# Moving the later modulation rows into the early stage, with raw weight blocks in two sets and side tokens loaded apart

## The chip, the cores and the metric

The kernel runs on one core of one Trainium2 chip. The metric is the device time in microseconds; lower is better. Before the change, three runs took 2741.22 to 2743.19 us, with a median of 2743.05. Another execution was profiled; it took 2743.47 us, and the profile's span, from its first to its last instruction, is 2741.7 us.

## The reference, cut to what matters

One layer of a diffusion trunk: an HGRN2 mixer (gated linear recurrence, both directions, 8 heads of 128) and a gated ConvFFN, each behind an RMSNorm that is modulated by rows made from `silu(c)`. 2048 latent tokens of width 1024, 256 context tokens.

```python
sc_lat, sc_ctx = jax.nn.silu(c), jax.nn.silu(c_ctx)
m_l = (sc_lat @ w_ada[l] + b_ada[l])[:, None, :]        # six rows of 1024
sh1, sc1, g1, sh2, sc2, g2 = jnp.split(m_l, 6, axis=-1)
hl = modulate(rmsnorm(lat, norm_g[l, 0]), sh1, sc1)
yc, yl = hgrn2_mixer(hc, hl, hg_w_in[j], ...)           # h @ w_in: q, f_fwd, f_bwd, i, g
lat = lat + g1 * yl
hl = modulate(rmsnorm(lat, norm_g[l, 1]), sh2, sc2)
lat = lat + g2 * conv_ffn(hl, ffn_w_up[l], ...)
return rmsnorm(lat, final_g)
```

The first two modulation rows (`sh1`, `sc1`) are needed at once. The change deals with the last four: `g1`, `sh2`, `sc2`, `g2`. `g1` is first needed in the mixer's second pass, where it scales the output weight; the others later.

## The kernel before, in words

The order of the instructions of each engine is drawn by a list scheduler at build time: an instruction that the text issues late can be put earlier on its queue when its operands and its place are free, loads above all. The text gives priorities through its order. It uses agendas: `at(when, f)` puts a step at a tick, and a tick passes with each three matmuls (one k step). Matrix products run with split operands: each fp32 factor is a high part (ScalarE, line 80) and a remainder (VectorE, line 81), and each k step multiplies high x high, high x low and low x high.

**Early stage** (`early()`, up to about 421 us). It makes the values (`ty` 3) and the output gates (`ty` 4) of all tokens by a Strassen-like scheme: seven products (`FACTORS`) for each pair of heads, of 12 matmuls each. `todo` is their order: 49 products over the second half of the tokens (`g` = 1 in the code), then, from `turn_over` on, 56 over the first half. A pair of heads is a `Heads` object: `prepare` loads the raw weight blocks (two of 512 KB, line 591), makes two sums on POOL (`sums`, lines 217 and 218) and splits the block that is needed, four products ahead (`LOOK`). Raw blocks lie in four first places (`rawp` twice, `Sf`, `Sb`), used once, and then in a ring of four in the pool `px`.

The token factors of the first half of the tokens come from `side_tokens`: four groups of two token tiles each are loaded (line 657), normalized (lines 130, 132), turned by TensorE (line 139), modulated on ScalarE (line 143), combined on VectorE and stored to `part_d` (line 664). All four groups use one tile, `side`; group j's load and norm are one step, at tick `c0 + 40 + 25 * j`, and its turns follow from 9 ticks later. `load_factor` (line 695) brings the parts back as factors into `fraw` and splits them. `turned_out` transposes a finished value (line 476) some ticks after its product and stores it.

**Mixer** (`mixer_scan()`, about 421 to 1250 us). Two passes over the 8 heads: the first over the first half of the tokens and the context, the second over the rest. Each unit projects gates and queries (lines 870 to 872), makes decay factors on VectorE, and steps the state (line 1070, VectorE) that TensorE reads for the outputs (line 1087).

The later modulation rows are a generator here, `ada_rest` (lines 1126 to 1154). For each of four rows it goes over 8 blocks of `w_ada` (512 KB each, line 1131), accumulates block x `silu(c)` on VectorE (lines 1143 and 1144), adds over partitions with two fp32 matmuls against ones (line 1151), and stores the row in `m_rows`. It steps 8 times in the second pass's first head and 6 times in each of the next five, each step tied behind the unit's last factor (`tied`). In heads 2 to 5, `gate1` and `out_scaled` (line 1170) make the scaled output weight from the first of these rows.

Of the kernel before, what the change touches and what calls it, by code (L numbers as in the profile page):

```python
# [21 lines left out]
D = 1024  # L22
# [23 lines left out]
def body(ctx, tc, a, out):  # L46
# [204 lines left out]
    def early():  # L251
# [143 lines left out]
        def then(f, *args):  # L395
            with behind_of(chain[-1]):
                chain.append(f(*args))
# [73 lines left out]
        def turned_out(o, dst, after=6):  # L471

            def turn():
                tr = z_tile("tr")
                for i in range(UT):
                    pe.transpose(tr[:, i], o[:, i], ident)
                act.activation(o, tr, AF.Copy)
                sp.dma_start(dst, o)

            at(clock[0] + after, turn)  # L480
# [8 lines left out]
        for k in range(KT):  # L489
            at(clock[0] + 36 + 4 * k, lambda k=k: then(unit0, k))  # L490
# [69 lines left out]
        raw_ring, raw_first = [], []  # L560

        def raw_tile():
            if len(raw_first) < 4:
                p, tag = ((rawp, "raw"), (rawp, "raw"), (hp, "Sf"), (hp, "Sb"))[len(raw_first)]
                raw_first.append(p.tile([128, 2, 4, 128], F32, name="raw", tag=tag,
                                        bufs=2 if p is rawp else 1))
                return raw_first[-1]
            if not raw_ring:
                raw_ring.extend([px.tile([128, 4, 2, 4, 128], F32, name="raw", tag="X", bufs=1), 0])
            raw_ring[1] += 1  # L570
            return raw_ring[0][:, (raw_ring[1] - 1) % 4]

        class Heads(Blocks):

            def __init__(self, ty, h):
                super().__init__(ring)
                self.ty, self.h, self.z, self.loaded = ty, h, {}, False
# [24 lines left out]
        at(c0 + 27, lambda: gs[2].first_half(lp.tile([128, D], F32, name="raw", tag="stg", bufs=1)))  # L602
# [4 lines left out]
        for i in (0, 2):  # L607
            todo += [(1, p, n) for n in FACTORS[2:] for p in vs[i:i + 2]]
            if i == 0:
                todo.insert(-9, (1, gs[2], "B21"))  # L610
                todo += [(1, gs[2], n) for n in ("T2", "T1", "T3", "B22", "T4")]
        todo += [(1, p, n) for n in FACTORS[2:] for p in gs[0:2]]
        turn_over = len(todo)
        for ty in (3, 4):
            for i in (0, 4):
                both = [Heads(ty, h) for h in (i, i + 2)]
                todo += [(0, p, n) for n in FACTORS for p in both]
# [26 lines left out]
        def side_tokens(j, now):  # L644
# [3 lines left out]
            xs, hs = [[side[0][:, 2 * i + u] for u in range(2)] for i in range(2)]  # L648
            hms = [h.rearrange("p (k n) -> p k n", k=KT) for h in hs]
# [28 lines left out]
            at(now, load)  # L678
            for i, (u, g) in enumerate(((0, 0), (0, 1), (1, 0), (1, 1))):
                at(now + 9 + 2 * i, lambda u=u, g=g: turn(u, g))  # L680
            at(now + 18, differences)
            at(now + 20, differences2)

        for j in range(UT):
            side_tokens(j, c0 + 40 + 25 * j)

        factor_raw = []
# [139 lines left out]
    def mixer_scan():  # L827
# [298 lines left out]
        def ada_rest():  # L1126

            def load(n):
                i, k = divmod(n, KT)
                raw = spare_raw()  # L1130
                sp.dma_start(raw, a["w_ada"][k * 128:(k + 1) * 128, (2 + i) * D:(3 + i) * D])
                return raw

            ahead = load(0)
            yield
            for i in range(4):
                acc_ = xp.tile([128, D], F32, name="acc", tag="xt", bufs=1)
                for k in range(KT):
                    raw = ahead
                    if KT * i + k + 1 < 4 * KT:  # L1140
                        ahead = load(KT * i + k + 1)
                    s_ = sil[:, k:k + 1]
                    tied(lambda: dve.scalar_tensor_tensor(acc_, raw, s_, acc_, OP.mult, OP.add)
                         if k else dve.tensor_scalar(acc_, raw, s_, None, OP.mult))
                    if k < KT - 1:
                        yield
                row = acc_[0:1]
                yield
                for n in range(2):
                    z = ps.tile([1, 512], F32, name="z", tag="pj", bufs=3)  # L1150
                    pe.matmul(z, ones, acc_[:, n * 512:(n + 1) * 512], start=True, stop=True)
                    act.activation(row[:, n * 512:(n + 1) * 512], z, AF.Copy)
                sp.dma_start(m_rows[i], row)
                yield

# [107 lines left out]
        rest = ada_rest()  # L1263
# [71 lines left out]
        for g in range(2):  # L1335
            for h in range(NH):
# [874 lines left out]
```

## Time and profile before

| What | Value |
|---|---|
| median of three runs | 2743.05 us |
| profiled execution, its own time | 2743.47 us |
| its span | 2741.7 us |
| PE busy | 2670.5 us, 97% |
| DVE (VectorE) busy | 2069.3 us, 75% |
| ACT (ScalarE) busy | 1165.8 us, 43% |
| POOL (GpSimd) busy | 668.1 us, 24% |
| HBM read and written | 331.51 and 159.66 MB, 179 GB/s |

A wait row reads "engine, tile written, line <- what it waited for: us in total, times, longest". A timeline row gives start, duration, engine, line, operation, out<-in, form, count, and in brackets the idle time before it. Matmuls are pipelined, so a matmul's own duration is longer than its share of TensorE's time.

### The profile page before, as it was taken

The page shows a single profiled execution, that of the slowest core. Times are in us where ns is not written, and L with a number is a line of the kernel's source. Part 1 is how long each engine was busy: PE and PEld are TensorE (multiplying, and loading weights), DVE is VectorE, ACT ScalarE, POOL GpSimd, SP SyncE. Part 2 cuts the span into 40 slices and gives each one's busy share as a digit, 9 for nine tenths or more (in the row PEclk, how much of TensorE's full clock was granted, in tenths as well). Part 3 has the DMA queues.
Part 4 walks back from the last instruction along what each step waited for, and adds up shares of the span by engine and source line. Part 5 has one row for each costly group of instructions (what it writes and reads, how often), then busy time and mean ns, then how long its engine had stood idle before and what let it go on. Part 6 is the DMA issues. An engine that isn't in the chain of part 4 may idle for free.

```text
span 2741.7 us, 41959 instructions
## 1 busy us (share of the span) xinstructions
PE 2670.5 (97%) x15880; PEld 2225.4 (81%) x15880; DVE 2069.3 (75%) x2941; ACT 1165.8 (43%) x1987; POOL 668.1 (24%) x956
## 2 busy tenths in 40 slices
PE   7889999999999999999999999999999999999998
PEld 4667888888888787888887888888888888888887
DVE  4767446777777888778987887777877787578896
ACT  4655343333332222235666444444544444333444
POOL 1433222222221222211210543433334440000001
PEclk9999999999999999999999999999999999999999
DMA  8667236344367565537889322228222224888663
GB/s 327 226 223 261 96 109 219 110 149 146 113 226 239 177 231 181 167 101 280 288 304 346 115 89 66 85 85 307 88 66 85 85 93 124 311 282 289 196 190 131
DMA packets 249826, 493.92 MB, mean 180 GB/s; under 512 B 27284, under 2 KB 140308, under 8 KB 239000
## 3 DMA queue, kind: packets, MB, share of 16 engines
q1 hardware_dynamic: 244904, 482.00, 52.3%
q10 hardware_dynamic: 4720, 9.24, 0.9%
q8 instruction: 125, 2.05, 0.3%
q14 instruction: 77, 0.63, 0.1%
HBM read 331.51 MB, written 159.66 MB: 179 GB/s over the span
## 4 chain that ended last, share of the span: by engine, by line
PE 78%; DVE 7%; DMA 1%; ACT 1%; issue 1%; POOL 1%; POOLq 0%; DVEq 0%; ACTq 0%; SPq 0%
PE z L872 6%; PE z L870 6%; PE z L871 6%; PE y L2024 5%; PE y L2025 5%; PE y L2023 5%; PE zc L1422 3%; PE zc L1424 3%; PE zc L1425 3%; PE za L1425 3%; PE za L1424 3%; PE zd L1425 3%; PE zd L1424 3%; PE zd L1422 3%; PE za L1422 3%; PE y L1526 2%
## 5 line engine op out<-in xcount | busy, mean ns | idle before, releaser
L81 DVE TENSOR_TENSOR w<-raw,w 128x512 fp32r<-128x512 f32 (+1 forms) x262 | 217.6, 834 | 85.5 <-ACT w L80 83.2
L80 ACT ACTIVATE w<-raw 128x512 fp32r<-128x512 f32 (+1 forms) x262 | 174.7, 672 | 177.7 <-PE zd L1425 76.1
L2024 PE MATMUL y<-w,mh 128*128 128x512 f32 x600 | 233.5, 389 | 0.3 <-DVE w L81 0.3
L2025 PE MATMUL y<-w,ml 128*128 128x512 f32 x600 | 233.4, 389 | 0.0
L2023 PE MATMUL y<-w,mh 128*128 128x512 f32 x600 | 233.2, 389 | 0.0
L81 DVE TENSOR_TENSOR w<-s,w 128x512 fp32r<-128x512 f32 x171 | 157.9, 927 | 78.6 <-ACT w L80 76.9
L870 PE MATMUL z<-tok,w 128*128 128x512 f32 x512 | 208.2, 407 | 0.0
L872 PE MATMUL z<-tok,w 128*128 128x512 f32 x512 | 200.2, 391 | 0.0
L871 PE MATMUL z<-tok,w 128*128 128x512 f32 x512 | 200.1, 391 | 0.0
L80 ACT ACTIVATE w<-s 128x512 fp32r<-128x512 f32 x171 | 106.7, 630 | 181.3 <-POOL s L218 80.8
L914 DVE TENSOR_TENSOR_SCAN S<-F,d 128x528 f32<-128x528 f32 (+1 forms) x80 | 91.5, 1145 | 111.0 <-ACT F L896 111.0
L217 POOL TENSOR_TENSOR s<-raw 128x512 f32<-128x512 f32 x57 | 90.4, 1587 | 229.7 <-DMA raw<-in_w_up_dram 133.7
L1422 PE MATMUL zc<-rT,w 128*128 128x512 f32 x352 | 137.0, 389 | 1.9 <-DMA rT<-rhs1T 1.9
L1424 PE MATMUL zc<-rT,w 128*128 128x512 f32 x352 | 136.9, 389 | 0.0
L1425 PE MATMUL zc<-rT,w 128*128 128x512 f32 x352 | 136.9, 389 | 0.0
L2024 PEld LDWEIGHTS y<-w,mh 128*128 128x128 f32 x600 | 112.6, 188 | 23.9 <-DVE w L81 0.8
L2023 PEld LDWEIGHTS y<-w,mh 128*128 128x128 f32 x600 | 112.6, 188 | 23.7 <-ACT w L80 0.3
L2025 PEld LDWEIGHTS y<-w,ml 128*128 128x128 f32 x600 | 112.6, 188 | 23.6
L76 POOL TENSOR_TENSOR rs<-rs,mhalf 128x1 f32<-128x1 f32 (+3 forms) x53 | 55.1, 1043 | 313.3 <-DVE rs L75 300.8
L1424 PE MATMUL za<-rB,w 128*128 128x512 f32 x336 | 130.7, 389 | 0.0
L1425 PE MATMUL za<-rB,w 128*128 128x512 f32 x336 | 130.7, 389 | 0.0
L1422 PE MATMUL za<-rB,w 128*128 128x512 f32 x336 | 130.7, 389 | 0.0
(457 smaller groups left out, 7660.8 us busy)
## 6 DMA issues: line engine op xcount, KB each, us to landing
w<-w SPq DMA_DIRECT2D x48, 1024.0 KB, 5.2
raw<-in_w_up_dram SPq DMA_DIRECT2D x88, 512.0 KB, 3.8
raw<-in_w_in_dram SPq DMA_DIRECT2D x67, 512.0 KB, 5.7
lr<-m SPq DMA_DIRECT2D x49, 512.0 KB, 5.1
m<-r SPq DMA_DIRECT2D x66, 256.0 KB, 4.1
spare<-in_w_ada_dram SPq DMA_DIRECT2D x32, 512.0 KB, 5.2
kq<-stash SPq DMA_DIRECT2D x15, 1024.0 KB, 7.7
og<-stash SPq DMA_DIRECT2D x30, 512.0 KB, 5.4
```

The lines of the kernel that those rows point to most:

```text
L80: i = act.activation(h, src, AF.Copy)
L81: j = dve.tensor_tensor(l, src, h.bitcast(F32), OP.subtract)
L870: pe.matmul(z, w[:, 0, k], h, start=k == 0, stop=False, skip_group_check=True)
L871: pe.matmul(z, w[:, 0, k], l, start=False, stop=False, skip_group_check=True)
L872: pe.matmul(z, w[:, 1, k], h, start=False, stop=k == KT - 1, skip_group_check=True)
L914: dve.tensor_tensor_scan(flat(S[:, d]), flat(F[:, d]), flat(d1[:, 0:ns]), 0.0, OP.mult, OP.max)
L1422: pe.matmul(o, w[:, 0, k], r[:, :, 0, k], start=start and k == 0, stop=False, skip_group_check=True)
L1424: pe.matmul(o, w[:, 0, k], r[:, :, 1, k], start=False, stop=False, skip_group_check=True)
L1425: i = pe.matmul(o, w[:, 1, k], r[:, :, 0, k], start=False, stop=k == 3, skip_group_check=True)
L2023: pe.matmul(z, lh, rh, start=start, stop=False, skip_group_check=True)
L2024: pe.matmul(z, lh, rl, start=False, stop=False, skip_group_check=True)
L2025: pe.matmul(z, ll, rh, start=False, stop=stop, skip_group_check=True)
```

## The change

- `ada_rest` moves from the mixer's second pass into the early stage's second half. Its 37 steps are put at ticks from `turn_over` + 16, 4 1/3 ticks apart. Blocks are loaded two steps ahead instead of one, the sum lies in the tile `stg`, and the rest is drained before the last `T2` of that half, ahead of the load of the factor `B12`.
- Raw blocks: two sets of four places, the four first places and the four in `px`, used in turns. Loads are issued for a pair, or for two pairs, at written-out places of `todo`, and the sums on POOL when the first T factor is prepared.
- Side tokens: load and norm are two steps. Loads are at ticks `c0` + 44, 73, 88, 98; norms at `c0` + 52, 81, 101, 121, the turns from 8 ticks after that. Groups 2 and 3 are loaded to raw places of the first set instead of `side`.
- Smaller ones: `turned_out` 8 ticks after the product instead of 6, the first unit's steps 2 ticks later, the third gate pair's first half loaded 6 ticks earlier, the first two factor loads 1 tick later.

```diff
-        def turned_out(o, dst, after=6):
+        def turned_out(o, dst, after=8):
...
-            at(clock[0] + 36 + 4 * k, lambda k=k: then(unit0, k))
+            at(clock[0] + 38 + 4 * k, lambda k=k: then(unit0, k))
...
+        def raw_tiles(x):
+            if not x:
+                return [p.tile([128, 2, 4, 128], F32, name="raw", tag=tag, bufs=2 if p is rawp else 1)
+                        for p, tag in ((rawp, "raw"), (rawp, "raw"), (hp, "Sf"), (hp, "Sb"))]
+            if not raw_x:
+                raw_x.append(px.tile([128, 4, 2, 4, 128], F32, name="raw", tag="X", bufs=1))
+            return [raw_x[0][:, i] for i in range(4)]
+
+        def load_raws(pairs, x):
+            tiles = raw_tiles(x) if isinstance(x, bool) else [raw_tiles(True)[i] for i in x]
+            for p in pairs:
+                p.raws([tiles.pop(0) for _ in range(2)])
+                for i, r in enumerate(p.raw):
+                    sp.dma_start(r.rearrange("p i k n -> p (i k n)"), a["w_in"][p.h + i, p.ty])
...
-                if not self.loaded and not (n in ("B11", "B21") and hasattr(self, "src")):
-                    self.loaded = True
-                    self.raws([raw_tile() for _ in range(2)])
-                    for i, r in enumerate(self.raw):
-                        sp.dma_start(r.rearrange("p i k n -> p (i k n)"), a["w_in"][self.h + i, self.ty])
+                if n[0] == "T" and not self.summed:
+                    self.summed = True
                     self.sums(pool, *[pb.tile([128, 4, 128], F32, name=n, tag=n) for n in ("s1", "s2")])
...
+        loads = {len(todo) - 5: (vs[0:2], False)}
+        loads[len(todo) - 11] = [gs[2]], (0, 1)
+        loads[len(todo) - 10] = [vs[2]], (2, 3)
+        loads[len(todo) - 4] = [vs[3]], (0, 1)
+        loads[len(todo) - 6] = gs[0:2], False
...
+        for i, (ty, h) in enumerate(((3, 0), (3, 4), (4, 0), (4, 4))):
+            both = [Heads(ty, h), Heads(ty, h + 2)]
+            loads[len(todo) - 12] = both, i % 2 == 0
+            todo += [(0, p, n) for n in FACTORS for p in both]
...
+            if j > 1:
+                xs = [p.tile([128, D], F32, name="x", tag=tag, bufs=n) for p, tag, n in
+                      (((rawp, "raw", 2), (rawp, "raw", 2)), ((hp, "Sf", 1), (hp, "Sb", 1)))[j - 2]]
...
+            def norm():
+                for u in range(2):
                     normalize(xs[u], hs[u], pb)
...
-            at(now, load)
+            load()
+            at(now, norm)
...
-            side_tokens(j, c0 + 40 + 25 * j)
+            at(c0 + (44, 73, 88, 98)[j], lambda j=j: side_tokens(j, c0 + 52 + (0, 29, 49, 69)[j]))
...
+            if i == turn_over:
+                for m in range(37):
+                    at(clock[0] + 16 + 4 * m + m // 3, lambda: next(rest, None))
+            if i in loads:
+                load_raws(*loads[i])
...
+                if g == 0 and n == "T2":
+                    for _ in rest:
+                        pass
+                    factor_raw.clear()
...
-                    at(c0 + 142 + 4 * (n == "B21"), lambda n=n: next_factor(n))
+                    at(c0 + 143 + 4 * (n == "B21"), lambda n=n: next_factor(n))
...
-                if g == 1 and h < NH - 2:
-                    n = 8 if h == 0 else 6
-                    for i in range(n):
-                        at(c + 3 + 46 * i // n, lambda: next(rest, None))
```

`ada_rest` itself, as it is now (cut):

```python
ahead = [load(n) for n in range(2)]
yield
for i in range(4):
    acc_ = lp.tile([128, D], F32, name="acc", tag="stg", bufs=1)
    for k in range(KT):
        raw = ahead.pop(0)
        ...  # acc_ = raw * s_ (+ acc_) on VectorE, no longer tied
        if KT * i + k + 2 < 4 * KT:
            ahead.append(load(KT * i + k + 2))
        yield
    for n in range(2):
        z = ps.tile([1, 512], F32, name="z", tag="tr")
        pe.matmul(z, ones, acc_[:, n * 512:(n + 1) * 512], start=True, stop=True)
        act.activation(row[:, n * 512:(n + 1) * 512], z, AF.Copy)
    sp.dma_start(m_rows[i], row)
    yield
```

More of the change, by code (lines that the diff above doesn't have):

```diff
@@ L558, in product @@
                 finished(g, p, *((0, 1) if n == "B22" else (1, 0)), o)
[L560 to L571, printed above, removed]
+        raw_x = []
+        def raw_tiles(x):
[11 more added lines that the diff above has]
+                    sp.dma_start(r.rearrange("p i k n -> p (i k n)"), a["w_in"][p.h + i, p.ty])
         class Heads(Blocks):
@@ L676, in differences2, with spare_raw, ada_rest, load @@
                 put(3)
[L678 removed]
+            load()
+            at(now, norm)
             for i, (u, g) in enumerate(((0, 0), (0, 1), (1, 0), (1, 1))):
[L680 to L682 removed]
+                at(now + 8 + 2 * i, lambda u=u, g=g: turn(u, g))
+            at(now + 17, differences)
+            at(now + 19, differences2)
         for j in range(UT):
[L685 removed]
+            at(c0 + (44, 73, 88, 98)[j], lambda j=j: side_tokens(j, c0 + 52 + (0, 29, 49, 69)[j]))
+        spare = []
+        def spare_raw():
+            if not spare:
+                spare.extend([hq.tile([128, 4, D], F32, name="spare", tag="cxt", bufs=1), 0])
+            spare[1] += 1
+            return spare[0][:, (spare[1] - 1) % 4]
+        def ada_rest():
+            def load(n):
+                i, k = divmod(n, KT)
+                raw = spare_raw()
+                sp.dma_start(raw, a["w_ada"][k * 128:(k + 1) * 128, (2 + i) * D:(3 + i) * D])
+                return raw
+            ahead = [load(n) for n in range(2)]
+            yield
+            for i in range(4):
+                acc_ = lp.tile([128, D], F32, name="acc", tag="stg", bufs=1)
+                for k in range(KT):
+                    raw = ahead.pop(0)
+                    s_ = sil[:, k:k + 1]
+                    if k:
+                        dve.scalar_tensor_tensor(acc_, raw, s_, acc_, OP.mult, OP.add)
+                    else:
+                        dve.tensor_scalar(acc_, raw, s_, None, OP.mult)
+                    if k == KT - 1:
+                        row = spare_raw()[0:1]
+                    if KT * i + k + 2 < 4 * KT:
+                        ahead.append(load(KT * i + k + 2))
+                    yield
+                for n in range(2):
+                    z = ps.tile([1, 512], F32, name="z", tag="tr")
+                    pe.matmul(z, ones, acc_[:, n * 512:(n + 1) * 512], start=True, stop=True)
+                    act.activation(row[:, n * 512:(n + 1) * 512], z, AF.Copy)
+                sp.dma_start(m_rows[i], row)
+                yield
+        rest = ada_rest()
         factor_raw = []
@@ L1124, in spare_raw @@
             return spare[0][:, (spare[1] - 1) % 4]
[L1126 to L1154, printed above, removed]
         g1s = []
```

18 lines of the change are left out of this document (6 added, 12 removed).

## The prediction

> **What bounds the kernel now.** I read the totals of the page first, then TensorE's own waits, then the busy time by stage, then the two places with waits in order of time. The totals:
>
> ```profile
> span 2741.7 us, 41959 instructions
> ...
> PE 2670.5 (97%) x15880; PEld 2225.4 (81%) x15880; DVE 2069.3 (75%) x2941; ACT 1165.8 (43%) x1987; POOL 668.1 (24%) x956
> ```
>
> TensorE is busy for all but 71 us. The change leaves every matmul in, so what it can gain is idle time of TensorE in the stages that it touches, and what it can cost is new idle time there. TensorE's waits between 80 and 1110 us (line, what it waited for, total, times, longest):
>
> ```profile
> PE o L1087 <- DVE states L1070: 12.7, 11, 1.5
> PE tp L139 <- ACT side L143: 9.2, 3, 5.1
> PE tp L139 <- DVE side L132: 5.1, 2, 3.0
> PE za L515 <- ACT u L544: 4.0, 1, 4.0
> PE tr L476 <- DVE hm L246: 2.2, 1, 2.2
> PE tr L299 <- DVE hm L246: 2.1, 1, 2.1
> PE za L515 <- ACT w L80: 1.9, 1, 1.9
> PE tr L476 <- DVE out L557: 1.1, 3, 0.5
> ```
>
> The first row lies in the mixer's second pass over the heads, the others in the early stage. The stages by window (length, busy time and instructions of PE, PEld, DVE, ACT, POOL, then granted clock, DMA share, GB/s):
>
> ```profile
> 110.00:130.00 20.00, 10.58 (x46) 8.03 (x46) 17.64 (x17) 15.45 (x33) 14.72 (x10) 0.80 0.75 262
> 170.00:190.00 20.00, 14.12 (x67) 11.17 (x66) 9.49 (x15) 12.46 (x28) 7.68 (x7) 0.91 0.67 219
> 260.00:270.00 10.00, 6.04 (x20) 4.54 (x19) 7.28 (x10) 5.09 (x11) 2.93 (x2) 0.83 0.91 294
> 270.00:420.00 150.00, 150.00 (x693) 124.04 (x692) 66.19 (x93) 57.07 (x95) 39.39 (x39) 1.00 0.35 116
> 850.00:1100.00 250.00, 238.55 (x2132) 197.78 (x2130) 207.93 (x299) 63.86 (x120) 51.05 (x120) 1.00 0.61 198
> 1102.00:1150.00 48.00, 48.00 (x427) 39.53 (x426) 33.72 (x51) 13.91 (x26) 10.66 (x25) 1.00 0.50 160
> ```
>
> Three things are to be seen. The early second half (270 to 420) has TensorE full and VectorE at 66 of 150. The mixer's second pass (850 to 1100) has VectorE at 208 of 250 (83%) and TensorE short by 11.5; from 1102 on, where no modulation rows run, VectorE is at 70% and TensorE is full. And in the three short windows TensorE loses more than its waits, since the granted clock is down to 0.80 to 0.91.
>
> **Modulation rows leave the mixer.** VectorE just before one of the eleven waits, and the matmul that waits:
>
> ```profile
> 1050.59 1.27 DVE L1143 SCALAR_TENSOR_TENSOR acc<-spare,sil,acc 128x1024 f32<-128x1024 f32 x1
> 1051.79 0.68 DVE L980 TENSOR_TENSOR qp<-qp,rt 128x512 f32<-128x512 f32 x1
> 1052.39 0.34 DVE L1070 SCALAR_TENSOR_TENSOR states<-states,sd,kv 128x128 f32<-128x128 f32 x1
> ```
> ```profile
> 1052.78 0.49 PE L1087 MATMUL o<-states,qi 128*128 128x128 f32 x2 [1.50 <-DVE states L1070]
> ```
>
> VectorE runs these without a gap, so the state update that TensorE lacks is late by every row step in front of it. Rows of the moved instructions, by tile and by line:
>
> ```profile
> L1131 SPq DMA_DIRECT2D spare<-in_w_ada_dram x32: 332/390/1025, 784.5 to 1072.5; - x32
> L1143 DVE SCALAR_TENSOR_TENSOR acc<-spare,sil,acc x28: 1270/1275/1283, 828.1 to 1099.1; 128x1024 f32<-128x1024 f32 x28
> ...
> DMA to landing us min/median/max: 2.6/4.2/9.1
> L1151 PE MATMUL z<-acc,ones x16: 590/592/592, 883.2 to 1103.9; 128*1 128x512 f32 x16
> ```
>
> One step is 1.275 us and no wait exceeds 1.5, so one step fewer ahead of each update removes the most part: the gain lies between about 10 and the whole 12.7. Several steps run per unit, so I take 12.7. The scaling of the output weight stays in this stage, with eight instructions in four heads; the 1102 window says that VectorE has room at 70%. The 16 row matmuls, at most 16 x 0.59 = 9.4 us, move with the rows: no change in the sum.
>
> **Modulation rows enter the early second half.** At most 32 x 1.275 = 40.8 us of VectorE come on top of 66.2 of 150: 71%, the level of the window without waits. A product is 12 matmuls; by 150/693 = 0.216 us each it is 2.6 us, and a tick (3 matmuls) 0.65. The 37 row steps span 160 ticks, 104 us, so one is due every 2.8 us and its load is issued two steps, 5.6 us, ahead. They move 32 x 0.524 = 16.8 MB, 161 GB/s on top of 116: 277, which the window at 294 shows to be possible. The cover is the sums' banks: the bank of T1 is written again three products later, 7.8 us. A load of 4.2 is in time; one of 9.1 is 3.5 late, and four times the row matmul then waits on TensorE's own queue for about 1.8. So 0 to 7 us; I take 1.5, near the median's end. Without the cover each late load would count in full (rival 3). The loads also stand in SyncE's queue between the stores of finished sums, and cost SyncE 32 x 0.39 = 12.5 us, which nothing waits for unless a load does.
>
> **Side tokens, later and loaded apart.** The four groups turn 11, 15, 10 and 5 ticks later (7, 10, 6.5 and 3 us), and groups 2 and 3 have raw places of their own instead of the side tile that the group before still stores from. ScalarE and TensorE at the longest of these waits:
>
> ```profile
> 122.06 5.35 ACT L143 ACTIVATE side<-tp,B,A 128x128 f32<-128x128 f32 x15
> 127.22 0.72 ACT L80 ACTIVATE w<-raw 128x512 fp32r<-128x512 f32 x1
> ```
> ```profile
> 127.98 0.80 PE L515 MATMUL za<-tok,w 128*128 128x512 f32 x1 [1.85 <-ACT w L80]
> 128.58 0.63 PE L517 MATMUL za<-tok,w 128*128 128x512 f32 x1
> ```
>
> The evictions come when ScalarE is late with the token splits, and the weight splits queue behind them; then TensorE runs at 0.63 a matmul. The waits on `side` are 9.2 + 5.1, and the weight wait behind them 1.9: 16.2 together. The delays are longer than the longest waits (5.1, 3.0), but VectorE is at 17.6 of 20 there, so some will return under another name. Between 0 and 16.2, I take 13. The clock: (1 - 0.80) x 20 + (1 - 0.91) x 20 = 5.8 us of clock lost, part of it while idle; I take 3. What is late next is the side stores of group 3, below.
>
> **Turned-out values two ticks later.** The transposes on L476 waited 2.2 + 1.1 = 3.3; two ticks are 1.3. Between 0 and 3.3, I take 1.6. The first unit's two ticks: the wait of 2.1 on L299 has the same late VectorE before and after, so 0 (bounds +1.3, -1.3).
>
> **Raw blocks in two sets.** More places mean earlier loads, and sums on POOL that come with the first T factor instead of with the load; the same loads and sums are issued, 0. One place is tight: the raws of the second gate pair go to the places that group 3 of the side tokens leaves. Rows of that chain (last turn before, first load after the part stores landed, landing of raws, POOL sum):
>
> ```profile
> 206.70 0.52 PE L139 MATMUL tp<-ident,side 128*128 128x128 f32 x3
> ```
> ```profile
> 217.48 0.59 SPq L695 DMA_DIRECT2D fraw<-part  x1
> ```
> ```profile
> DMA to landing us min/median/max: 3.4/4.2/8.8
> L218 POOL TENSOR_TENSOR s<-s,raw 128x512 f32<-128x512 f32 x9 | 14.1, 1569 | 1.3 <-DVE w L81 0.8
> ```
>
> 10.8 from the last turn to the stores' landing, 4.2 for the load, 2 x 1.57 for the sums, some 1.3 for the split (0.72 on ScalarE above, less on VectorE): 19.4 us. The last turn is now 25 ticks (16.3 us) ahead of that pair's T2. So 3 us late, 0 if transposes between stretch the ticks, and 7.7 with the slowest load; I take 1.5, midway to the median's case. The same stores also gate the factor loads for the second half, due one tick later. There ScalarE sits in front of a split and the eviction that TensorE needs waits behind it:
>
> ```profile
> 262.04 0.63 ACT L80 ACTIVATE rT<-fraw 128x512 fp32r<-128x512 f32 x1 [1.74 <-DMA fraw<-part]
> ```
>
> The 4.0 of L515 <- L544 and (1 - 0.83) x 10 = 1.7 of clock belong to it. I leave it as it is: 0, with -5.7 if the splits come in another order and +3 if the stores' 5 ticks pass through. The mixer's first raw weights, fetched far ahead before, now wait for the early stage's last pair to leave its places, four products (10.4 us) before the first mixer matmul; 4.2 and two splits fit, so 0, or 2 with a load of 8.8.
>
> **Sum.** -12.7 - 13 - 3 - 1.6 + 1.5 + 1.5 = -27.3. The profiled execution took 2743.47, 0.4 over the median of 2743.05; from the median that makes 2715.8, so 2716.
>
> **Rivals.** 1: the early stage's waits only change their names, since ScalarE and VectorE have the same work there (17.6 of 20 in the window at 110); then the mixer's 12.7 remains: 2730. Against it stand the windows at 170 with VectorE at 9.5 of 20, where the wait is for a load and a norm. 2: all goes, the turn-over too: -12.7 - 16.2 - 5.8 - 3.3 - 1.3 - 5.7 = -45.0, 2698; no row shows VectorE so free before 260. 3, slower: the row loads choke the early second half. SyncE's waits between 270 and 420:
>
> ```profile
> SPq L478 <- ACT out L477: 51.8, 12, 10.7
> SPq L527 <- ACT out L526: 42.7, 16, 7.0
> ```
>
> A load behind such a store starts late. With two loads ahead, a step can't be shorter than half of a load's time from due to landed. At 9.1 it is 4.55 instead of 2.8: 32 x 1.75 = 56, less the cover of 7.8, 48 lost: 2743 - 28.8 + 48 = 2762. It decides from the point where (L/2 - 2.8) x 32 - 7.8 exceeds 28.8, at L = 7.9 us; the median of 4.2 speaks against. The Trainium skill, "DMA: Bandwidth & Descriptors", in the section on the anatomy of one DMA, states the same cause: a semaphore wait happens on the issuing sequencer, before the DMA is dispatched, not in the DMA engines. By that rule each of SyncE's waits shown would delay the loads behind it, and the time would be rival 3's; the trace has the waits, but no row of before has row loads among them. 4: the states are late without the rows too (the other VectorE work simply fills in): -14.6, 2728; the 1102 window speaks against.
>
> **Chances.** Forecast, within some 10 us (2708 to 2727): 0.5. Rival 1 with rival 4: 0.2. Rival 2: 0.15. Rival 3: 0.08. Two or more of the upper bounds together (7 + 7.7 + 3), which leaves the time where it was: 0.07. The range goes from rival 2 to the edge of those last: 2698 to 2738. A measurement tells 0.2%, 5.5 us, from no change: faster 0.85, same 0.07, slower 0.08.
>
> **What would show it.** Right: no wait of L1087 on L1070 in the second pass, VectorE near 70% there and in the early second half with TensorE still full, waits on `side` below 4 us, granted clock back to 1.0 at 110 to 190. Wrong: waits of the early products on ScalarE or VectorE with row steps in front, row steps that wait for their loads, a wait on the second gate pair's T2, or a wait at the change to the mixer.

## The result, and the profile after

| | before | after |
|---|---|---|
| median of four runs each | 2743.12 us | 2718.28 us (2716.44 to 2719.17) |
| ratio, 95% interval | 1 | 0.9908 [0.9891, 0.9925] |
| profiled execution, its span | 2741.7 us | 2717.5 us |

The kernel is 24.8 us faster, 0.9%. The forecast was 2716 (2698 to 2738). The total came out right and the way to it only in part: the rows brought more than forecast, the early stage less. The totals of the page after:

```profile
span 2717.5 us, 41952 instructions
...
PE 2665.1 (98%) x15880; PEld 2224.9 (82%) x15880; DVE 2077.1 (76%) x2941; ACT 1162.8 (43%) x1987; POOL 679.9 (25%) x956
```

TensorE's waits after in the early stage, from the list of the whole span (the rows left out belong to the start-up and the ConvFFN; of the 2.2 on L299 <- L477, 0.7 lie behind 60 us, the rest in the start-up):

```profile
PE tr L476 <- DVE out L557: 4.9, 1, 4.9
PE tp L139 <- ACT side L143: 3.6, 2, 3.3
PE za L515 <- ACT u L544: 3.0, 1, 3.0
PE za L515 <- DVE u L546: 2.4, 1, 2.4
PE tr L299 <- ACT out L477: 2.2, 2, 1.5
PE tr L476 <- DVE hm L246: 2.0, 1, 2.0
PE zd L515 <- DVE out L549: 2.0, 1, 2.0
...
PE za L515 <- ACT w L80: 1.5, 1, 1.5
PE tr L299 <- DVE hm L246: 1.0, 1, 1.0
```

The state update is L1133 now and the outputs L1150: no wait between them is left of the 12.7 us. In the early stage the waits on `side` fell from 14.3 to 3.6 (5.0 in a second profile of the same kernel, after_again below), but three others stand there, on VectorE's results: 4.9 on L557, where before had 1.1 in three pieces, 2.4 on L546 and 2.0 on L549, which before did not have. The stages after, by window (columns as before; the mixer's windows are moved ahead by 20 us with the stage):

```profile
110.00:130.00 20.00, 14.90 (x55) 11.45 (x54) 18.01 (x17) 14.67 (x32) 14.53 (x9) 0.71 0.88 304
170.00:190.00 20.00, 18.05 (x83) 14.58 (x82) 11.45 (x19) 14.17 (x33) 5.49 (x6) 0.91 0.62 213
260.00:270.00 10.00, 10.00 (x48) 8.24 (x46) 7.11 (x8) 4.98 (x10) 6.77 (x4) 1.00 0.89 333
270.00:420.00 150.00, 150.00 (x671) 118.00 (x670) 105.62 (x130) 56.41 (x96) 45.64 (x37) 1.00 0.61 202
830.00:1080.00 250.00, 250.00 (x2316) 214.85 (x2315) 191.69 (x291) 65.53 (x122) 56.31 (x132) 1.00 0.46 152
1082.00:1130.00 48.00, 47.97 (x431) 40.95 (x430) 36.10 (x54) 12.64 (x23) 11.57 (x27) 1.00 0.51 160
```

The early second half took the row steps (VectorE 66 to 106 of 150) with TensorE full. The mixer's second pass has TensorE full (238.55 to 250.00 of 250) and VectorE at 77%. At 110 to 130 the granted clock did not come back to 1.0: it is 0.71, after 0.80. Part of that fall is where the window ends: over 110 to 140 us it is 0.83 before and 0.81 after.

**Where the time went.** Starts of single instructions cut each trace into stretches: A from the first early product to the first matmul of a `T2` of the second tokens, B on to `turn_over`, C on to the mixer's first matmul, D on to the first output matmul after the second pass. What lies ahead of A varies between executions by up to 4 us and is left out of the reading; behind D all kernels lie between 1498.8 and 1503.1.

| stretch, us | A | B | TensorE idle in B | granted clock in B | C | D |
|---|---|---|---|---|---|---|
| before | 64.9 | 126.7 | 10.5 | 0.97 | 165.9 | 819.6 |
| after | 62.4 | 126.8 | 9.2 | 0.96 | 171.5 | 796.0 |
| rows_alone | 64.8 | 124.9 | 6.9 | 0.95 | 173.1 | 795.8 |
| rows_back | 62.4 | 122.8 | 7.1 | 0.97 | 160.1 | 819.8 |
| nosums | 60.1 | 113.0 | 0.2 | 0.99 | 169.2 | 796.0 |
| side_old | 62.4 | 121.2 | 5.2 | 0.97 | 172.1 | 796.0 |
| ring_old | 62.4 | 115.2 | 1.9 | 0.99 | 174.3 | 795.8 |
| both_old | 62.4 | 123.4 | 6.1 | 0.96 | 177.4 | 796.1 |
| late_raws | 62.4 | 120.4 | 6.3 | 0.98 | 172.3 | 796.0 |
| sums_dve | 62.4 | 113.2 | 0.5 | 0.99 | 177.6 | 796.0 |
| ring_turn | 62.4 | 115.7 | 1.9 | 0.98 | 172.2 | 795.8 |
| ring_turn_dve | 62.4 | 113.7 | 0.0 | 0.98 | 169.1 | 795.8 |
| after_again | 62.4 | 128.8 | 9.2 | 0.93 | 170.0 | 796.0 |

Before to after: A -2.5, B 0, C +5.6, D -23.6. The whole gain shows in the mixer, and the 126.7 us of B, in which three of the four groups of side tokens are worked off, did not shrink. Two executions of the changed kernel differ by 2.0 us in B and 1.5 in C, so smaller differences of B or C say little. What makes B long is idle time of TensorE and lost clock alone: B less the idle time, and less B times what the clock lacks to 1, is an estimated 110.6 to 112.5 us in every row of the table.

### The profile page after: what moved, and what is told of

Same layout as the page of the kernel before. It is cut to its first block, busy times and chain, and to the rows that moved or that the text cites. A ratio compares the mean times of both kernels' runs of the same rounds, so it can differ in the third digit from the quotient of the medians.

```text
span 2717.5 us, 41952 instructions
## 1 busy us (share of the span) xinstructions
PE 2665.1 (98%) x15880; PEld 2224.9 (82%) x15880; DVE 2077.1 (76%) x2941; ACT 1162.8 (43%) x1987; POOL 679.9 (25%) x956
## 4 chain that ended last, share of the span: by engine, by line
PE 87%; DVE 1%; DMA 1%; issue 0%; ACT 0%; POOL 0%; ACTq 0%; SPq 0%; POOLq 0%; DVEq 0%
PE z L935 7%; PE z L934 7%; PE z L933 7%; PE y L2052 5%; PE y L2053 5%; PE y L2051 5%; PE zc L1450 3%; PE zc L1453 3%; PE zc L1452 3%; PE za L1453 3%; PE zd L1453 3%; PE zd L1450 3%; PE za L1452 3%; PE zd L1452 3%; PE za L1450 3%; PE kv L1130 2%
## 5 line engine op out<-in xcount | busy, mean ns | idle before, releaser
L1136 ACT ACTIVATE sk<-kv 128x256 f32<-128x256 f32 x64 | 24.6, 384 | 248.4 <-DVE states L1133 152.0
```

## The experiments

Open after the result were: how much of the 24.8 us is the rows' and how much the rest's; why stretch B stayed as it was although its longest waits went; and which part brings the new waits. One theory was that VectorE sets B, because its remainders (line 81) run slower beside the sums on POOL, so that a wait taken away comes back under another name. The rivals were the order of ScalarE's work, the ticks of the side tokens, and the loads of the raw blocks. All edits are against the changed kernel unless said otherwise. Ratios are to the kernel before on the same chip.

**rows_alone and rows_back: the rows apart from the rest.** rows_alone is the kernel before with `ada_rest` moved as in the change, and nothing else. rows_back is the changed kernel with `ada_rest` in the mixer again.

```diff
# rows_alone, against the kernel before
+            if i == turn_over:
+                for m in range(37):
+                    at(clock[0] + 16 + 4 * m + m // 3, lambda: next(rest, None))
...
-                        at(c + 3 + 46 * i // n, lambda: next(rest, None))
...
```

> The kernel before with one part of the change: the modulation rows run in the early stage's second half (same 37 steps, tile stg, drain before the last T2); raw ring, side tokens and turned-out values as before. Theory A (the mixer is nearly the whole gain, the early stage gave little): TensorE's 12.7 us of waits on the state update go and about 3.5 more of the mixer's small losses, nothing else changes: 2743 - 16 = 2727, between 2723 and 2730. Theory B (the prediction: side tokens, clock and transposes are worth some 17 of the gain): 2743 - 12.7 + 1.5 = 2732, and the other parts make the rest.

> The changed kernel with the modulation rows back in the mixer's second pass as before (one block ahead, tied, tile xt); raw sets, side tokens and all smaller edits stay. Theory A: the eleven waits of the state update return (12 to 13 us, up to 1.5 each) and the time is 2718 + 16 = 2734 to 2738. Theory B: the other parts carry 13 to 15 of the gain, so the time is 2718 + 12.7 = 2731 or less, with rows_alone no better than 2730. The sum of the two gains against the gain of both tells whether the parts depend on each other.

Measured: rows_alone 2723.35, 0.9936 [0.9924, 0.9949], 17.1 us below its before of 2740.47; rows_back 2731.30, 0.9970 [0.9959, 0.9982], 9.2 below. Together 26.3, against 24.8 for the whole: the parts add up. In rows_back the mixer's wait is there again as it was, its one row between 270 and 1130 us:

```profile
PE o L1103 <- DVE states L1086: 12.7, 11, 1.5
```

rows_alone has +7.2 in stretch C and -23.8 in D. The 7.2 are the row matmuls themselves: 16 records at some 0.45 us. In the trace after, four of them take TensorE from 294.25 to the product's next matmul at 296.05, 1.80 us:

```profile
294.25 1.88 PE L735 MATMUL z<-acc,ones 128*1 128x512 f32 x4
296.05 0.50 PE L515 MATMUL zc<-rT,w 128*128 128x512 f32 x1
```

So the row steps, their loads and their stores cost the second half nothing beyond their matmuls, to within the 1 us by which the wait at the turn-over differs (4.0 before, 2.9 here). D is shorter by 23.8: 7.2 of matmuls, 12.7 of waits, and about 3.9 that stood in no wait row. Nearly all of the 3.9 lies at the same place: counted from the start of the matmul before, the steps into the 192 matmuls that read the states add up to 41.6 us before and 25.2 after, which is 16.3 less and not 12.7. A wait row begins only where the profile lets the matmul before it end. rows_back gives one more number: C is 160.1, 5.8 less than before. Without the rows, the rest of the change takes the wait at the turn-over away whole; with the rows, a part is there (on L544, 3.0 after and 1.3 in after_again).

**nosums: is it the sums on POOL?** The early stage's sums of raw blocks are left out, so that the products work with plain blocks.

```diff
+            def sums(self, eng, s1, s2):
+                self.src.update(S1=self.src["A21"], S2=self.src["A22"], S3=self.src["A11"], S4=self.src["A12"])
```

> The changed kernel without the sums of raw weight blocks on POOL in the early stage (the splits read plain blocks instead; the computation leaves these sums out). Theory A2: the early stage's remaining waits come from VectorE, whose 128x512 remainders take 1.77 instead of 0.68 us while POOL works (24 of them in the first half, 21.8 us); without the sums most of that goes, TensorE's waits between 100 and 262 us (19 us) fall below 8 and the time falls by 8 to 15 us: 2703 to 2710. Rival: the waits come from the order of the queues or from landing times; then the time stays within 4 us of 2718.

Measured: 2702.97, 0.9867 [0.9852, 0.9882], 37.5 below, where the change itself is 24.8 below its own before. B falls from 126.8 to 113.0. The full-size remainders between 60 us and the turn-over that take more than 0.8 us number 23 after, for 21.3 us in excess of 0.685 each, and 5 here, for 4.2. VectorE's groups between 60 and 260 us, first after, then nosums:

```profile
L81 DVE TENSOR_TENSOR w<-raw,w 128x512 fp32r<-128x512 f32 x24 | 21.8, 912 | 3.5 <-ACT w L80 3.5
...
L81 DVE TENSOR_TENSOR rT<-hm,rT 128x512 fp32r<-128x512 f32 x16 | 17.5, 1115 | 4.8 <-ACT rT L80 4.8
```
```profile
L81 DVE TENSOR_TENSOR w<-raw,w 128x512 fp32r<-128x512 f32 x54 | 37.1, 699 | 8.2 <-ACT w L80 8.0
L81 DVE TENSOR_TENSOR rT<-hm,rT 128x512 fp32r<-128x512 f32 x16 | 13.1, 835 | 6.2 <-ACT rT L80 6.1
```

The same instruction takes 0.70 us on average where POOL makes no sums and 0.91 where it does. Some 13 us of the early stage hang on the sums (37.5 against 24.8). nosums leaves out the slowing of VectorE, POOL's time and the sums' latency at once, so it does not say by itself which of them counts.

**tie0: do the ticks of the first group decide?** The first group's transposes are bound behind the last matmul of the product at their tick.

```diff
+                if j in (0,):
+                    with tc.issue_after(last_mm[0]):
+                        transpose_mod(xs[u], hms[u], g, ps, A1[0], B1[0], "tr", 2, True)
+                    return
...
```

> The changed kernel with group 0's sixteen side transposes tied on TensorE behind the last matmul before them in the text, so that they really stand 11 ticks later in the queue. Theory C (the written ticks did not move them: the queue has them at the same product as before, so the same wait of 3.3 us stays): the wait on side at 119 us goes, the weight split that followed (1.5) shrinks too, 3 to 5 us less: 2713 to 2715. Rival: ScalarE and VectorE are late there anyhow; the products behind wait as long instead, and the time stays within 1.5 us of 2718.

Measured: 2714.00, 0.9904 [0.9891, 0.9918]: the changed kernel's ratio, within the intervals. The 2714 us are in the range named for theory C only because before is faster on this chip too (2740.47). TensorE's longest waits in tie0, whose lines stand 2 and 3 further down (L517 is L515 of the changed kernel, L560 is L557):

```profile
PE za L517 <- ACT w L80: 7.6, 1, 7.6
PE tr L476 <- DVE out L560: 4.2, 1, 4.2
```

No wait on `side` is left, and its place is taken by one of 7.6 on a weight split that ScalarE does late. So taking these evictions out of the way won nothing: TensorE waits for ScalarE at that place either way. In the change itself these transposes had not moved: their "11 ticks later" is a priority only, and on TensorE's queue of both kernels they stand ahead of the same matmul.

**side_old, ring_old, both_old: side tokens against raw sets.** side_old has the side tokens as before, ring_old the raw places of before (four first places, then a ring of four, loaded with the first factor), both_old both; the rows stay moved and the small edits stay.

```diff
# side_old
...
-            at(c0 + (44, 73, 88, 98)[j], lambda j=j: side_tokens(j, c0 + 52 + (0, 29, 49, 69)[j]))
+            side_tokens(j, c0 + 40 + 25 * j)
...
# ring_old
...
-                if n[0] == "T" and not self.summed:
-                    self.summed = True
+                if not self.loaded and not (n in ("B11", "B21") and hasattr(self, "src")):
+                    self.loaded = True
+                    self.raws([raw_tile() for _ in range(2)])
...
-            if i in loads:
-                load_raws(*loads[i])
```

> The changed kernel with the side tokens as before (one tile, load and norm in one step at c0 + 40 + 25 j, turns 9 ticks later, factor loads at 142). The parts beside the rows were worth some 8 to 9 us together. Theory S (the side tokens carry most of it): the waits on side return to 9 to 14 us in total and the ratio to the kernel before goes from 0.991 to about 0.994. Rival R (the raw sets carry it): the ratio stays within 0.001 of 0.991 and the waits on side change their size but are paid elsewhere.

> The changed kernel with the raw blocks as before: four first places used once, then the ring of four in px, loads and POOL sums when a pair is first prepared. Theory S: the ratio stays within 0.001 of 0.991; the wait of 4.9 us of a turned-out value on VectorE near 227 us, which only the kernels with two sets show, goes. Rival R: the ratio goes to 0.994, and the wait at the turn-over grows from 3.0 towards 4.0 us with its clock.

> Rows moved and the small edits (turned-out values and first unit 2 ticks later, third gate pair's first half 6 earlier); side tokens and raw ring as before. It splits what ring_old has over rows_alone (the stretch from the first T2 to the turn-over took 115.2 us in ring_old, 124.9 in rows_alone, 126.7 before). Theory D (the side tokens' own places are worth it, and the two raw sets take it back): that stretch is 122 to 126 us and the ratio to the kernel before 0.992 to 0.994. Rival (the small edits do it): the stretch is 115 to 118 and the ratio 0.989.

Measured, with raw places by row and side tokens by column, each against the kernel before on its own chip:

| | side tokens as before | side tokens changed |
|---|---|---|
| raw places as before | both_old 0.9932 [0.9920, 0.9944] | ring_old 0.9888 [0.9874, 0.9903] |
| raw places changed | side_old 0.9903 [0.9889, 0.9918] | after 0.9908 [0.9891, 0.9925], again 0.9918 [0.9904, 0.9931] |

both_old stands at rows_alone's 0.9936: the small edits bring nothing that can be measured. From there the side tokens alone bring 12 us and the raw sets alone 8, both with intervals apart from both_old's. Both together bring 4 to 7, which the intervals do not tell apart from nothing: the gains don't add. Their places differ, as the stretches show. The side tokens shorten B (both_old 123.4, ring_old 115.2). The raw sets shorten C (177.4 and 172.1). One row of each shows it, both_old and side_old:

```profile
PE za L515 <- ACT u L544: 6.5, 1, 6.5
```
```profile
PE za L515 <- ACT u L544: 1.9, 1, 1.9
```

And with both, B is back at 126.8 and, in after_again, 128.8.

**late_raws: is it the early load of the first value raws?** In the changed kernel the raws of the first pairs after the turn-over are loaded while B still runs, and here their load comes later, bound behind a factor load.

```diff
...
-            loads[len(todo) - 12] = both, i % 2 == 0
+            loads[len(todo) - (8 if i == 0 else 12)] = both, i % 2 == 0, i == 0
...
```

> The changed kernel with one set of loads later: the raws of the second half's first two pairs are issued 8 products instead of 12 ahead of the turn-over and tied on SyncE behind the last factor load. Theory A2 (POOL sums of these pairs, 33 us ahead of their need, slow five VectorE remainders from 0.68 to 1.75 us just when an output is due): the wait of 4.9 us at 227 falls below 2 and the time by 2 to 5 us. Rival: the output is late from VectorE's queue order alone; the wait stays at 4 or more and the time within 1.5 us.

Measured: 2714.99, 0.9903 [0.9887, 0.9920]; the time is not told apart from the changed kernel's. The wait is: 4.9 becomes 1.7, and 0.9 and 0.8 turn up that were not there.

```profile
PE tr L476 <- DVE out L557: 1.7, 1, 1.7
```

The timeline shows how the 4.9 arises. First VectorE after, then POOL after, then TensorE after, then VectorE in late_raws around the same value:

```profile
221.32 3.46 DVE L81 TENSOR_TENSOR w<-raw,w 128x512 fp32r<-128x512 f32 x2
224.71 1.74 DVE L81 TENSOR_TENSOR rB<-fraw,rB 128x512 fp32r<-128x512 f32 x1
226.37 0.68 DVE L557 TENSOR_TENSOR out<-u,zc 128x512 f32<-128x512 f32 x1
```
```profile
220.81 1.75 POOL L217 TENSOR_TENSOR s<-raw 128x512 f32<-128x512 f32 x1
222.63 1.60 POOL L223 TENSOR_TENSOR raw<-raw 128x512 f32<-128x512 f32 x1
224.20 1.70 POOL L217 TENSOR_TENSOR s<-raw 128x512 f32<-128x512 f32 x1
```
```profile
227.19 0.84 PE L476 MATMUL tr<-ident,out 128*128 128x128 f32 x4 [4.86 <-DVE out L557]
```
```profile
217.92 1.28 DVE L81 TENSOR_TENSOR w<-raw,w 128x512 fp32r<-128x512 f32 x2
219.12 0.68 DVE L81 TENSOR_TENSOR rB<-fraw,rB 128x512 fp32r<-128x512 f32 x1
219.72 0.67 DVE L557 TENSOR_TENSOR out<-u,zc 128x512 f32<-128x512 f32 x1
```

With POOL at its sums, three remainders take 5.1 us (221.32 to 226.37); without, 1.8 (217.92 to 219.72). The value that TensorE turns stands behind them. So most of this wait comes from the early raw loads, by way of the POOL sums that follow them. B is 120.4 here and 115.2 in ring_old; of these 5.2 us, 4.4 are idle time of TensorE, in the 1.7 that is left of this wait and in another, of 2.6 on L546, which ring_old does not have and which is followed below.

**sums_dve: the sums on VectorE.** All early sums but those of the second half go to VectorE.

```diff
...
-                    self.sums(pool, *[pb.tile([128, 4, 128], F32, name=n, tag=n) for n in ("s1", "s2")])
+                    self.sums(self.eng, *[pb.tile([128, 4, 128], F32, name=n, tag=n) for n in ("s1", "s2")])
...
```

> The changed kernel with the sums of raw blocks of the first half's pairs on VectorE instead of POOL (the second half's stay on POOL). POOL no longer slows VectorE there (21 us of slowed remainders in the first half), but 28 sums of 0.69 us, 19 us, come on top of it, with less latency (0.69 instead of 1.6 a sum). Theory A2 in its strong form (the slow remainders cost more than the sums): 2 to 6 us less than the changed kernel. Rival (VectorE's total counts): no gain, 0 to 5 us more.

Measured: 2712.78, 0.9894 [0.9880, 0.9909]. The slowed remainders fall to 11 (9.0 us in excess), B to 113.2, and the wait on L557 to 0.5. But at the turn-over 6.3 come up, and C is 177.6:

```profile
PE za L515 <- ACT u L544: 6.3, 1, 6.3
```

So 13.6 us of B are won and 6.1 of C lost; by the intervals the net gain on the changed kernel isn't certain. B is as short as in nosums (113.0), though VectorE now makes those sums itself and is busy for 87.7 of the 113.2 us (74.7 in nosums). So it is not VectorE's amount of work that made B long.

**ring_turn, ring_turn_dve, after_again: the pieces put together.** ring_turn is ring_old with the splits of one factor put behind the eviction that TensorE waits for at the turn-over. ring_turn_dve is ring_turn with the sums on VectorE as in sums_dve. after_again is the changed kernel once more, on the same chip.

```diff
# ring_turn, against ring_old
...
+            def split_late(j):
+                with tc.issue_after(evicted[-1]):
+                    split(f[:, j, 0], f[:, j, 1], raw[:, j])
...
+                if n in ('T4',):
+                    at(clock[0] + 17 + j, lambda j=j: split_late(j))
+                else:
+                    at(clock[0] + 9 + j, lambda j=j: split(f[:, j, 0], f[:, j, 1], raw[:, j]))
```

> The changed kernel with the raw ring as before, and the split of the last token factor (T4) 8 ticks later and tied on ScalarE behind the eviction of the first product after the turn-over. Theory E (at the turn-over ScalarE stands in front of that split, waiting for the factor's load, while the eviction that TensorE needs is queued behind it): the wait of za on u falls from 4.2 to below 1, with 1.7 of clock behind it: 4 to 6 us less than ring_old, ratio about 0.987. Rival: the eviction is late for another reason, or the T4 product then waits for its factor; ratio 0.989.

> As ring_turn, and the first half's sums of raw blocks on VectorE instead of POOL (the stretch from T2 to the turn-over was 113.2 us with that and two raw sets, where the plain changed kernel had 126.8). Theory A2 (slowed remainders cost more than the sums): another 2 to 8 us less than ring_turn, ratio 0.984 to 0.986. Rival: ring_old has already what this gives (115.2); within 2 us of ring_turn.

> The changed kernel once more, unchanged, on the chip of the other three, so that ring_turn and both_old are compared with it there. 0.991 of the kernel before; if the raw sets cost what ring_old showed, it is 3 to 6 us slower than ring_old's ratio of 0.9888 gives, and its waits near 227 us on a turned-out value (4.9) are there again.

Measured: ring_turn 2708.13, 0.9879 [0.9864, 0.9894]; ring_turn_dve 2705.33, 0.9865 [0.9852, 0.9879]; after_again 2719.17, 0.9918 [0.9904, 0.9931]. In ring_turn the wait at the turn-over is 2.0, where ring_old has 4.2. The edit adds two lines, so the eviction of L544 is L546 in this kernel:

```profile
PE za L515 <- ACT u L546: 2.0, 1, 2.0
```

So the wait is halved, where theory E had it below 1; what else holds that eviction is not shown. The 2.2 less are the 2.1 us by which C is shorter (174.3 to 172.2), too little to be seen in the times. ring_turn_dve beats both kernels: 37 us below before, 14 below the changed kernel on the same chip, with intervals that don't touch. Against ring_turn and ring_old the intervals overlap, so what the sums on VectorE add there isn't certain. Of TensorE's waits from 60 us on it keeps these (L546 is again the eviction):

```profile
PE tp L139 <- ACT side L143: 3.6, 2, 3.3
PE tr L476 <- DVE hm L246: 2.0, 1, 2.0
PE za L515 <- ACT w L80: 1.5, 1, 1.5
PE tr L299 <- DVE hm L246: 0.9, 1, 0.9
PE tr L299 <- ACT out L477: 0.8, 1, 0.8
PE za L515 <- ACT u L546: 0.5, 1, 0.5
```

**The three new waits in B, kernel by kernel.** The lines are those of the changed kernel; a dash stands where no wait is listed.

| wait of TensorE, us | after, after_again | rows_back | late_raws | side_old | ring_old | both_old | nosums | sums_dve |
|---|---|---|---|---|---|---|---|---|
| on L546 | 2.4, 2.7 | 0.4 | 2.6 | 2.9 | - | - | - | - |
| on L549 | 2.0, 2.0 | 2.0 | 2.0 | - | 1.9 | - | - | - |
| on L557 | 4.9, 4.5 | 4.7 | 1.7 | - | - | - | 0.2 | 0.5 |

The wait on L546 goes with the raw sets (rows_back has little of it, 0.4), the one on L549 with the changed side tokens, and the long one on L557 only with both. Where POOL makes no sums for these tokens (nosums, sums_dve), at most 0.5 us of them is left. How the 2.4 arises can be seen in VectorE and TensorE after, then in VectorE in ring_old at the same operations:

```profile
129.08 1.78 DVE L683 TENSOR_TENSOR side<-side 128x512 f32<-128x512 f32 x1
...
134.19 1.75 DVE L687 TENSOR_TENSOR side<-side 128x512 f32<-128x512 f32 x1
135.86 0.68 DVE L546 TENSOR_TENSOR u<-u,za 128x512 f32<-128x512 f32 x1
```
```profile
136.59 0.50 PE L515 MATMUL za<-rT,w 128*128 128x512 f32 x1 [2.42 <-DVE u L546]
```
```profile
127.50 0.68 DVE L680 TENSOR_TENSOR side<-side 128x512 f32<-128x512 f32 x1
...
129.31 0.68 DVE L684 TENSOR_TENSOR side<-side 128x512 f32<-128x512 f32 x1
129.91 0.67 DVE L546 TENSOR_TENSOR u<-u,za 128x512 f32<-128x512 f32 x1
```

Three differences of the side tokens and one remainder stand ahead of L546 in both kernels. After, with four POOL sums of the early loaded blocks from 128.57 to 135.38, they take 6.8 us; in ring_old, where POOL still waits for its blocks until 134.93, 2.4. The amount of slowed work does not tell the two kernels apart: in B, 13 remainders are slowed by 11.6 us together after, and 15 by 11.4 in ring_old, with POOL busy for 46.1 and 45.7 us. What tells them apart is which result of VectorE stands behind the slowed ones. The 2.0 on L549 is of another kind: VectorE sits idle for 2.8 us until POOL has made the row scale (L76) for a norm (L132, 173.33) that stands ahead of L549 (175.47) on its queue.

## Why the prediction was right, and where it was not

By the steps of the sum:

- **Mixer, -12.7 taken; right in mechanism, too small in size.** All 12.7 went. D is shorter by another 3.9 beyond that and the matmuls. VectorE with 83% in the second pass cost TensorE more than its wait rows told. VectorE's share is 77% now, not near 70% as the signs named had it; TensorE is full all the same.
- **Row matmuls, 0.** They cost 7.2 in C and gave 7.2 in D. Right, with 7.2 for the bound of 9.4.
- **Row steps in the early second half, +1.5 taken.** Measured 0, to within 1 us: rows_alone has C longer by the 7.2 alone. The 32 loads landed in 3.3/4.7/6.8 us (minimum, median, maximum), VectorE waited 3.7 us for them in all, and TensorE not at all. The prediction's 2.6/4.2/9.1 is of every DMA on the tile `spare`; the row loads alone had 3.5/5.2/9.1 before, a median that is still in time for the 5.6 us of two steps. VectorE's share of 70% (105.62 of 150) is what the prediction worked out; the 202 GB/s stay under its 277. That settles rival 3. SyncE's longest waits after, between 270 and 430 us, still have the stores in front; behind them the row loads (L714) wait for their places:

```profile
SPq L527 <- ACT out L526: 37.6, 16, 4.4
SPq L478 <- ACT out L477: 26.3, 12, 3.2
SPq L714 <- DVE acc L725: 18.8, 14, 2.8
```

  The rule of the Trainium skill that stood beside that rival ("DMA: Bandwidth & Descriptors", the anatomy of one DMA) is stated there for DMAs that GpSimd issues; it agrees with where these waits stand on SyncE, on the issuing queue. Its consequence did not reach TensorE. That the two loads ahead are what covered it is likely, but no run loads one ahead here. The rows' net is thus about -17 by rows_alone, where the sum had -11.2.
- **Side tokens, -13 taken.** This is the step that failed. Its rows fell as forecast, from 16.2 to 5.1 (3.6 on `side`, 1.5 on the weights). But 4.9, 2.4 and 2.0 came up behind them, and B is as long as before: of this stretch's 126.7 nothing went. The prediction had the reason in hand, VectorE at 17.6 of 20 at 110, and let only 3.2 us return. Within B the idle time only went from 10.5 to 9.2. It went wrong in two places. It took a written tick for a place on the queue. And it priced the side tokens by themselves, while the raw sets put POOL's sums beside their differences and beside the remainders ahead of two results that TensorE needs (L546, L557): with the raw places of before the step is worth 12 us (both_old to ring_old, stretch B -8.2).
- **Raw sets, 0 with +1.5 for the second gate pair taken.** The second gate pair shows no wait. A cost came elsewhere, in B: the waits on L557 and L546, 4.9 and 2.4, stand behind VectorE work that POOL's early sums slowed. The prediction put the sums at nothing because the same sums are issued; their number is the same, their place is not. Raw sets alone bring 8 us; on top of the changed side tokens they cost 5 to 8 (0.9888 against 0.9908 and 0.9918; the second interval lies just apart, the first overlaps).
- **Clock, -3 taken.** Measured 0. The granted clock at 110 to 140 went from 0.83 to 0.81, at 170 to 190 it stayed at 0.91, and over 60 to 270 us it is 0.95 in both traces:

```profile
60.00:270.00 210.00, 183.98 (x891) 149.52 (x891) 148.32 (x200) 125.23 (x246) 76.86 (x54) 0.95 0.70 236
```
```profile
60.00:270.00 210.00, 189.08 (x908) 154.06 (x906) 151.05 (x198) 127.22 (x251) 80.45 (x56) 0.95 0.71 249
```

- **Turned-out values and the first unit, -1.6 taken.** By both_old against rows_alone nothing measurable: A is 2.4 shorter there, and C 4.3 longer.
- **Turn-over, 0 taken.** Without the rows -5.8, the lower bound named (-5.7); with them about 1 to 3 of the 4.0 are still there.

So -27.3 was made of -11.2 for the rows and -16.1 for the rest; measured are about -17 and -9. Rival 1 is right for most of the early stage and too small for the mixer. The two errors have opposite signs, and they hid each other in the total: that it came out within 3 us of the forecast is luck. One sum does not come out: the upper bounds 7, 7.7 and 3 together, in place of 1.5, 1.5 and 0, leave a gain of 12.6 us (2730) and not the time where it was, so they don't reach the range's end at 2738.

## What to carry to other kernels

Work that only has to be done sometime belongs in the stage where its engine is idle: 32 steps of 1.3 us cost nothing at a VectorE share of 44%, and at 83% they had cost TensorE more than its wait rows named. Before a wait is booked as a gain, ask which engine is late behind it, since the wait goes to the next instruction of that engine. When work moves to another time, look at what it then runs beside, and which result stands in the queue behind that: the same POOL sums, made earlier, cost here what the side tokens had won. And of two edits in one stage, measure each with and without the other: here each helped alone, and together one took back the other's gain.

## What the runs showed of the hardware

A VectorE remainder of 128x512 takes 0.68 us alone. All 23 that took over 0.8 us after, from 60 us to the turn-over, had a POOL sum or difference beside them; 17 of them took 1.68 to 1.79 and six 1.10 to 1.35, and POOL's additions stretch too, from 1.28 in the trace of before at 219 us to between 1.60 and 1.75 in the rows above. The Trainium skill, "SBUF — State Buffer", section "SBUF: two separate sides", says that the two engines take turns on one port pair, held for the whole instruction, and that a VectorE operation with two SBUF inputs is among those that must wait when the POOL operation reads SBUF. The timelines agree with the waiting: 1.74 is 0.68 and most of a POOL instruction. They agree with the turns too: the remainder that starts at 219.01, 0.16 us ahead of a POOL sum, keeps its 0.68, and the sum takes 1.68. They also show that the price is paid by the queue behind it: the 4.9 us hung on an operation of 0.68 us that was itself not slowed.

A row step (128x1024) was stretched too: the longest took 2.31 us in the early second half, against 1.28 at most in the mixer before. POOL ran beside each of the seven that took over 1.35 us; in nosums, without the sums, none of the 28 took so long.
